# A decoder block's gated recurrence: TensorE's order in the heads written out, VectorE's share in pieces, keys by a backward scan

## The chip, the cores and the metric

The kernel runs on one core of a Trainium2 chip, whose engines (TensorE, VectorE, ScalarE, GpSimd and SyncE) each work through an instruction stream of their own in order and wait for each other by semaphores. The metric is the device time of one execution in microseconds; the time of a kernel is the median of several executions.

## The reference

One decoder block for a sequence of 1024 tokens, 1024 channels wide, all in float32:

```python
proj = x @ w_in          # -> q, f, i, o_gate, pool_v, gate_a, gate_b
qf = silu(q) * 128 ** -0.5
f  = lb + (1 - lb) * sigmoid(f_pre);  k = 1 - f
# per head, 8 heads of 128: S_t = diag(f_t) S_{t-1} + k_t v_t^T ;  o_t = S_t^T q_t
o = hgrn2_chunked(qf, k, i, log f)
a = (rms_norm(o) * hgrn_norm_g * sigmoid(o_gate)) @ w_a
b = per_group_linear(causal_mean_w(pool_v) - pool_v) * pool_scale     # windows 2, 4, 8, 16
x = layer_norm(alpha * x + (sigmoid(gate_a) * a + sigmoid(gate_b) * b) @ w_out)
x = layer_norm(alpha * x + relu(x @ w_up) ** 2 @ w_down)
```

The recurrence is a scan over tokens, but inside a chunk it can be written with matrix products of queries, keys and values, each scaled by products of the decays `f` from the chunk's start to the token or from the token to the chunk's end.

## The kernel before

Every large product is made of three TensorE products of rounded parts (a high and a low part of each operand: high x high, high x low, low x high), and 2x2 block products are made of seven block products in place of eight. `pair` describes such a set of seven: two weight blocks of 128 columns against the two halves (512 tokens each) of the input. Each of its steps makes a weight operand (`w_part`: ScalarE rounds it to the high part, line 118, VectorE subtracts for the low part, line 119) and then issues 12 matmuls of 128x512 (`prod`, lines 201 to 204) into one PSUM bank. Sums between banks are taken by `copied` and `added` (lines 271 and 275). The weight operands sit in a ring of ten tiles, `w`. `run` issues the steps of a pair one after the other.

The heads stage runs after the value columns of the first projection. Its pairs are `head_inputs(h)` (q and f of head h), `output_gates(h)` (gates of two heads), `gates(j)` (the two merge gates) and `pooled(g)` (pooled input of group g, with its running means on VectorE). Between them stands `hgrn(h, u, ...)`, the recurrence of head h, half u (512 tokens, four chunks of 128, sub-blocks of 16):

- VectorE scans `f` forward within each sub-block for the running decay `fd` (line 811), takes its reciprocal (line 817), and makes from them the scaled queries and keys; ScalarE copies parts of them; GpSimd makes the small tables of decays (`T`, `p32`, `p64`, `dec`, `eq`, `ek`).
- TensorE transposes the keys to the chunk's end (line 870), forms the chunk states (line 875), the scores (lines 887 and 898) and the outputs (lines 915 and 918). VectorE chains the states (line 883) and copies the scores under a mask into `att` (line 905).
- ScalarE makes the norm (lines 923, 924 and 928, with a reciprocal on VectorE at line 925); TensorE transposes the result back (line 931), VectorE multiplies it by the gate in tile `og` (line 932), and SP's queue writes it to DRAM as `o` (line 933).

Tiles come from rings with a fixed number of buffers, named in `RINGS`; a new tile waits until the last use of the oldest one in its ring is over. All loads and stores of this stage are issued by SyncE (SP) in its own order. `o_sums(kp)` loads four finished halves of `o`, makes four sums and stores them.

After the last head come `pool_products(g)`, for g = 0 to 3: for each half it loads two pooled blocks (into rings `og` and `v`), splits them, and multiplies them with the group's pool weights (24 matmuls of 128x512 a group, lines 105 to 107). `gates(5)` to `gates(7)` are traced among them. Then the merge begins (products with `w_a`, then `w_out`, the layer norms and the MLP), which the change leaves alone.

What sets the order: the kernel is traced in program order, and a scheduler orders the instructions of each engine by the time that its own model foresees, with priorities where the kernel gives them. So before the change the recurrence's small matmuls fall between the matmuls of the pairs wherever the scheduler puts them.

Of the kernel before, what the change touches and what calls it, by code (L numbers as in the profile page):

```python
# [9 lines left out]
F32 = mybir.dt.float32  # L10
# [6 lines left out]
P = 128  # L17
# [12 lines left out]
PRIO_LAST = 3000  # L30
# [13 lines left out]
def tile_hybrid_block(  # L44
# [311 lines left out]

    def run(*pairs, made=(), behind=()):


        for i, steps in enumerate(zip(*pairs)):  # L360
            made_now = list(made[i]) if made else []
            if made_now:
                made_now.pop(0)()
            with tc.issue_after(made_last[behind[i]]) if behind and behind[i] else nullcontext():
                ws = [{operand: operand() for operand in operands} for operands, _ in steps]
            for n in range(len(ws[0])):
                if made_now:
                    made_now.pop(0)()
                for w, (_, products) in zip(ws, steps):
                    operand, product = products[n]  # L370
                    product(w[operand])

# [245 lines left out]
    with tc.tile_pool(name="tmp", bufs=1, side="right", reuse_waits="tile") as tmp:  # L618
# [3 lines left out]
        att = [hgp.tile([P, CH, P], F32, name=f"att{i}") for i in range(1)]  # L622
        for t in att:
            G.memset(t, 0.0)
# [6 lines left out]
        RINGS = dict(q=3, f=3, og=2, v=2, tA=2, tC=2, st=2)  # L631
# [11 lines left out]
        def head_inputs(h, behind=()):  # L643
            fs, qs = [None, None], [None, None]
# [23 lines left out]
            return fs, qs  # L668
# [39 lines left out]
        def pool_products(g):  # L708
# [6 lines left out]
            raw = raw_tile().rearrange("p k n c -> p (k n c)")[:, : 2 * 2 * P].rearrange("p (k c) -> p k c", c=2 * P)  # L715
# [90 lines left out]
        def hgrn(h, u, ft, q, v, og, state):  # L806

            fd = tt("tA")
            for i in range(2):
                w = slice(i * QUARTER, (i + 1) * QUARTER)  # L810
                V.tensor_tensor_scan(fd[:, w], starts.rearrange("p b s -> p (b s)"), ft[:, w], 1.0, ALU.max, ALU.mult)
            k = ft
            A.activation(k, ft, AF.Identity, bias=cmask[:, P - 1 : P], scale=-1.0)
            r = tt("tC")
            for i in range(CH):
                w = slice(i * P, (i + 1) * P)
                V.reciprocal(r[:, w], fd[:, w])  # L817
            T = small("T", [P, NB])
            G.tensor_copy(T, blk(fd)[:, :, SUB - 1])
            T2 = T.rearrange("p (b e) -> p b e", e=2)  # L820
            p32 = small("p32", [P, CH, 4])
            p32f = p32.rearrange("p c b -> p (c b)")
            G.tensor_mul(p32f, T2[:, :, 0], T2[:, :, 1])
            p64 = small("p64", [P, CH, 2])
            p32p = p32f.rearrange("p (b e) -> p b e", e=2)
            G.tensor_mul(p64.rearrange("p c e -> p (c e)"), p32p[:, :, 0], p32p[:, :, 1])
            dec = small("dec", [P, CH])
            G.tensor_mul(dec, p64[:, :, 0], p64[:, :, 1])
            eq = small("eq", [P, CH, 4])
            G.memset(eq[:, :, 0:1], 1.0)  # L830
            G.tensor_copy(eq[:, :, 1], p32[:, :, 0])
            G.tensor_copy(eq[:, :, 2], p64[:, :, 0])
            G.tensor_mul(eq[:, :, 3], p64[:, :, 0], p32[:, :, 2])
            ek = small("ek", [P, CH, 4])
            G.memset(ek[:, :, 3:4], 1.0)
            G.tensor_copy(ek[:, :, 2], p32[:, :, 3])
            G.tensor_copy(ek[:, :, 1], p64[:, :, 1])
            G.tensor_mul(ek[:, :, 0], p64[:, :, 1], p32[:, :, 1])


            V.tensor_mul(q, q, fd)
            kc = tt("tD")
            V.tensor_mul(kc, k, r)
            kr = tt("tE")
            V.tensor_mul(blk(kr), blk(kc), bc(T, [P, NB, SUB]))
            A.copy(pairs_of(kc)[:, :, 0], pairs_of(kr)[:, :, 0])
            qc = tt("tF")
            A.copy(pairs_of(qc)[:, :, 1], pairs_of(q)[:, :, 1])
            V.tensor_mul(
                pairs_of(qc)[:, :, 0], pairs_of(q)[:, :, 0],  # L850
                bc(pairs_of(r)[:, :, 0, SUB - 1], [P, NB // 2, SUB]),
            )
            V.tensor_mul(pairs_of(q)[:, :, 1], pairs_of(q)[:, :, 1], bc(T2[:, :, 0], [P, NB // 2, SUB]))
            V.tensor_mul(pairs_of(kr)[:, :, 0], pairs_of(kr)[:, :, 0], bc(T2[:, :, 1], [P, NB // 2, SUB]))
            q64 = hgp.tile([P, CH, 2, 32], F32, tag="q64", name=nm("q64"))
            k64 = hgp.tile([P, CH, 2, 32], F32, tag="k64", name=nm("k64"))
            A.copy(q64[:, :, 0], half64(q, 1)[:, :, 0])
            V.tensor_mul(q64[:, :, 1], half64(q, 1)[:, :, 1], bc(p32[:, :, 2], [P, CH, 32]))
            A.copy(k64[:, :, 1], half64(kr, 0)[:, :, 1])
            V.tensor_mul(k64[:, :, 0], half64(kr, 0)[:, :, 0], bc(p32[:, :, 1], [P, CH, 32]))  # L860
            qi = tt("tA")
            b32 = lambda t: t.rearrange("p (b s) -> p b s", s=32)
            V.tensor_mul(b32(qi), b32(q), bc(eq.rearrange("p c b -> p (c b)"), [P, 16, 32]))
            ke = tt("tC")
            V.tensor_mul(b32(ke), b32(kr), bc(ek.rearrange("p c b -> p (c b)"), [P, 16, 32]))


            pt = ps_tile("tr", 2)
            for c in range(CH - u):
                PE.transpose(pt[:, c * P : (c + 1) * P], ke[:, c * P : (c + 1) * P], ident)  # L870
            ket = tt("tH")
            A.copy(ket[:, : (CH - u) * P], pt[:, : (CH - u) * P])
            ds = ps_tile("hg", 2)
            for c in range(CH - u):
                PE.matmul(ds[:, c * P : (c + 1) * P], ket[:, c * P : (c + 1) * P], v[:, c], start=True, stop=True)
            st = tt("st")
            for c in range(CH - u):
                o = st[:, c * P : (c + 1) * P]
                if state is None and c == 0:
                    V.tensor_copy(o, ds[:, 0:P])  # L880
                else:
                    prev = state[:, 3 * P :] if c == 0 else st[:, (c - 1) * P : c * P]
                    V.scalar_tensor_tensor(o, prev, dec[:, c : c + 1], ds[:, c * P : (c + 1) * P], ALU.mult, ALU.add)


            def score(part, lo, keys, queries):
                PE.matmul(sc[part : part + 32, lo : lo + queries.shape[-1]], keys, queries, start=True, stop=True)

            for c in range(CH):
                for b in range(4):  # L890
                    lo = c * P + b * 32
                    score(b * 32, lo, kc[:, lo : lo + 32], qc[:, lo : lo + 32])
            for c in range(CH):
                for b in (0, 2):
                    lo = c * P + b * 32
                    score(b * 32, lo + 32, kr[:, lo : lo + 32], q[:, lo + 32 : lo + 64])
            for c in range(CH):
                PE.matmul(
                    sc[0:64, c * P + 64 : (c + 1) * P],
                    k64[:, c].rearrange("p a b -> p (a b)"),  # L900
                    q64[:, c].rearrange("p a b -> p (a b)"),
                    start=True, stop=True,
                )
            at = att[(2 * h + u) % 1]
            V.copy_predicated(
                at, cmask.bitcast(U32).unsqueeze(1).to_broadcast([P, CH, P]),
                sc.rearrange("p (c t) -> p c t", t=P),
            )


            o = ps_tile("hg", 2)
            for c in range(CH):
                w = slice(c * P, (c + 1) * P)
                first = state is None and c == 0
                PE.matmul(o[:, w], at[:, c], v[:, c], start=True, stop=first)
                if not first:
                    prev = state[:, 3 * P :] if c == 0 else st[:, (c - 1) * P : c * P]
                    PE.matmul(o[:, w], qi[:, w], prev, start=False, stop=True)
            ss = small("ss", [P, CH])
            on = tt("tH")  # L920
            for c in range(CH):
                w = slice(c * P, (c + 1) * P)
                A.activation(on[:, w], o[:, w], AF.Square, accum_out=ss[:, c : c + 1])
            A.activation(ss, ss, AF.Sqrt, bias=eps_rms, scale=1.0 / P)
            V.reciprocal(ss, ss)
            for c in range(CH):
# [20 lines left out]
        for h in range(HEADS):  # L947
            fs, qs = nxt
            state = None
            for u in range(2):  # L950
# [6 lines left out]
                if h + 1 < HEADS and u:  # L957
                    nxt = head_inputs(h + 1)
                    if h % 2:
                        output_gates(h + 1)  # L960
# [441 lines left out]
```

## Time and profile before

| | |
|---|---|
| median of 3 runs | 1462.83 us (1462.3 to 1464.97) |
| profiled execution | 1460.19 us |
| its span, first to last instruction | 1458.5 us |
| mean granted TensorE clock | 0.996 |
| heads stage, about | 118 to 600 us |

The profile is of one execution. Line numbers in it are those of the kernel before. "PE" is TensorE, "DVE" VectorE, "ACT" ScalarE, "POOL" GpSimd and "SP" SyncE; `out<-in` names the tiles that an instruction writes and reads; the number before a comma in a group's row is its busy time in us, the one behind it the mean duration in ns.

### The profile page before, as it was taken

The numbers are of one execution on the slowest core, as the hardware profiler recorded it, in microseconds if no ns is written. First come the engines' busy times: TensorE is split into PE (matmuls) and PEld (weight loads), VectorE is DVE, ScalarE is ACT, GpSimd is POOL, SyncE is SP. The second block draws the span as 40 slices with busy tenths as digits, with TensorE's granted clock in tenths as the row PEclk, the third lists the DMA queues.
The fourth block names the chain that finished last, engine by engine and source line by source line (L and its number), as shares of the span: only waits on it lengthen the run. The fifth ranks groups of instructions, "written<-read, shape, count | busy, mean of one in ns | idle before, by whom it ended". The sixth has DMA issues, their size and how long they took to land.

```text
span 1458.5 us, 20662 instructions
## 1 busy us (share of the span) xinstructions
PE 1436.4 (98%) x7377; PEld 1187.9 (81%) x7377; DVE 1141.6 (78%) x1838; ACT 758.3 (52%) x1383; POOL 58.6 (4%) x244
## 2 busy tenths in 40 slices
PE   8999999999999998999999999999999999999997
PEld 7888888888888886788888878888888888888886
DVE  5967989899898885768985597666666787777977
ACT  5445565666656655556542376555555443333535
POOL 0001001001000010000002100000000100000000
PEclk9999999999999999999999999999999999999999
DMA  7232233323234447897672225444474874445322
GB/s 253 70 126 87 85 98 101 109 75 114 90 99 138 152 132 249 301 299 241 223 247 99 73 94 195 159 146 144 152 261 149 275 260 150 153 141 163 130 73 116
DMA packets 160615, 226.82 MB, mean 156 GB/s; under 512 B 11232, under 2 KB 84480, under 8 KB 160512
## 3 DMA queue, kind: packets, MB, share of 16 engines
q1 hardware_dynamic: 158576, 218.93, 44.7%
q0 software_dynamic: 1152, 4.19, 0.8%
q10 hardware_dynamic: 784, 2.38, 0.5%
q8 instruction: 58, 0.95, 0.3%
q14 instruction: 45, 0.37, 0.1%
HBM read 154.16 MB, written 71.30 MB: 155 GB/s over the span
## 4 chain that ended last, share of the span: by engine, by line
PE 94%; DVE 3%; DMA 1%; ACT 1%; issue 0%; SPq 0%; DVEq 0%
PE ps_pj L201 16%; PE ps_pj L203 16%; PE ps_pj L204 16%; PE ps_pj L1283 4%; PE ps_pj L1285 4%; PE ps_pj L1284 4%; PE ps_pj L106 3%; PE ps_pj L107 3%; PE ps_pj L105 2%; PE ps_tr L1285 1%; PE ps_tr L1283 1%; PE ps_tr L1284 1%; PE ps_sc L201 1%; PE ps_sc L203 1%; PE ps_sc L204 1%; PE ps_hg L203 1%
## 5 line engine op out<-in xcount | busy, mean ns | idle before, releaser
L201 PE MATMUL ps_pj<-act,w 128*128 128x512 f32 x1068 | 421.6, 395 | 0.4 <-ACT act L123 0.2
L203 PE MATMUL ps_pj<-act,w 128*128 128x512 f32 x1068 | 415.1, 390 | 0.5 <-DVE act L124 0.5
L204 PE MATMUL ps_pj<-act,w 128*128 128x512 f32 x1068 | 414.1, 390 | 0.0
L201 PEld LDWEIGHTS ps_pj<-act,w 128*128 128x128 f32 x1068 | 200.6, 188 | 42.8 <-ACT act L123 0.6
L204 PEld LDWEIGHTS ps_pj<-act,w 128*128 128x128 f32 x1068 | 200.5, 188 | 42.3
L203 PEld LDWEIGHTS ps_pj<-act,w 128*128 128x128 f32 x1068 | 200.6, 188 | 40.6 <-DVE act L124 0.9
L118 ACT CAST w<-t 128x512 fp32r<-128x512 f32 x170 | 104.7, 620 | 105.0 <-PE ps_pj L203 53.8
L118 ACT CAST w<-raw 128x512 fp32r<-128x512 f32 x143 | 88.2, 620 | 117.3 <-PE ps_pj L203 62.5
L119 DVE TENSOR_TENSOR w<-raw,w 128x512 fp32r<-128x512 f32 x143 | 99.8, 702 | 55.2 <-ACT w L118 53.9
L119 DVE TENSOR_TENSOR w<-t,w 128x512 fp32r<-128x512 f32 x170 | 115.9, 685 | 29.6 <-ACT w L118 29.4
L1245 ACT CAST act<-act 128x1024 fp32r<-128x1024 f32 x66 | 66.9, 1050 | 107.9 <-issue 35.0
L1246 DVE TENSOR_TENSOR act<-act,act 128x1024 fp32r<-128x1024 f32 x66 | 79.3, 1220 | 18.5 <-ACT act L1245 15.8
L1285 PE MATMUL ps_pj<-act,act 128*128 128x512 f32 x240 | 92.9, 389 | 0.0
L1284 PE MATMUL ps_pj<-act,act 128*128 128x512 f32 x240 | 92.9, 389 | 0.0
L1283 PE MATMUL ps_pj<-act,act 128*128 128x512 f32 x240 | 92.4, 389 | 0.0
L275 DVE TENSOR_TENSOR c<-c,ps_pj 128x512 f32<-128x512 f32 x95 | 64.5, 681 | 18.0 <-PE ps_pj L204 13.4
L271 ACT COPY c<-ps_pj 128x512 f32<-128x512 f32 x96 | 55.2, 582 | 12.8 <-PE ps_pj L204 12.8
L817 DVE RECIPROCAL tC<-tA 128x128 f32<-128x128 f32 x64 | 54.1, 904 | 0.0
L1284 PEld LDWEIGHTS ps_pj<-act,act 128*128 128x128 f32 x240 | 45.1, 188 | 9.4
L1285 PEld LDWEIGHTS ps_pj<-act,act 128*128 128x128 f32 x240 | 45.1, 188 | 9.4
L1283 PEld LDWEIGHTS ps_pj<-act,act 128*128 128x128 f32 x240 | 45.1, 188 | 9.3
L241 DVE TENSOR_TENSOR t<-raw,raw 128x512 f32<-128x512 f32 x43 | 29.6, 689 | 21.9 <-DMA raw<-in_w_in_dram 19.7
(415 smaller groups left out, 2719.8 us busy)
## 6 DMA issues: line engine op xcount, KB each, us to landing
h<-c SPq DMA_DIRECT2D x106, 256.0 KB, 2.1
act<-h SPq DMA_DIRECT2D x78, 256.0 KB, 2.9
raw<-in_w_in_dram SPq DMA_DIRECT2D x64, 256.0 KB, 3.4
draw<-in_w_down_dram SPq DMA_DIRECT2D x16, 1024.0 KB, 7.8
raw<-in_w_up_dram SPq DMA_DIRECT2D x30, 512.0 KB, 4.2
raw<-in_w_in_dram SPq DMA_DIRECT2D x18, 512.0 KB, 4.0
hf<-h SPq DMA_DIRECT2D x34, 256.0 KB, 2.9
c<-o SPq DMA_DIRECT2D x24, 256.0 KB, 3.4
```

Of the source, the lines that this page charges most:

```text
L118: A.copy(hi, src)
L119: V.tensor_sub(lo, src, f(hi))
L201: PE.matmul(ps, wh[:, k], th, start=first and k == 0, stop=False, skip_group_check=True)
L203: PE.matmul(ps, wh[:, k], tl, start=False, stop=False, skip_group_check=True)
L204: PE.matmul(ps, wl[:, k], th, start=False, stop=k == CH - 1, skip_group_check=True)
L271: A.copy(t, ps)
L275: V.tensor_add(t, t, ps)
L1245: A.copy(hi, src)
L1246: V.tensor_sub(lo, src, f(hi))
L1283: PE.matmul(ps, hh[:, w], wh, start=fresh and n == 0, stop=False, skip_group_check=True)
L1284: PE.matmul(ps, hh[:, w], wl, start=False, stop=False, skip_group_check=True)
L1285: PE.matmul(ps, hl[:, w], wh, start=False, stop=n == M - 1, skip_group_check=True)
```

## The change

1. **Recurrence in parts.** `hgrn` becomes a class `Half` with methods: `prepare` (VectorE's, ScalarE's and GpSimd's share, a generator in six pieces), `turn_keys`, `scores`, `far_queries`, `states`, `load`, `outputs`, `turn_outputs`. A generator `recurrence` steps through all 16 halves. For half n TensorE's work stands in two groups: first the outputs of half n-1 with the key transposes and scores of half n, then four turns later the output transposes of n-1 with the states of n.
2. **TensorE's order.** After `head_inputs(0)` the rest of the stage is traced under a manual schedule for TensorE: its instructions keep the order in which they are traced. `run` advances the recurrence by one turn after each product of a pair; a half takes 8.5 turns on the mean. `ORDER` lists the pairs. After `ORDER` and the last turns come `pool_products(0)`, `gates(6)`, `pool_products` 1 to 3 and `gates(7)`.
3. **Keys by a backward scan.** The decay from each token to its sub-block's end, `to_end`, is scanned from `f` with negative steps; the keys are `k * to_end`. The four reciprocals of 128 columns and two products of 512 columns go; a reciprocal of the 32 sub-block ends and a product of 256 columns come.
4. **Rings.** `f` 3 to 4, `og` 2 to 1, `tC` 2 to 1, `tH` 1 to 2; the pool weights are loaded to a `tA` tile, not to a `raw` tile.
5. The raised priority of the last half goes.

```diff
-PRIO_LAST = 3000
+PER_HALF = 8.5
+TURN_BACK = 4
+TURNS_AHEAD = 3
+ORDER = (
+    ("inputs", 1), ("pooled", 0), ("inputs", 2), ("gates", 0), ("output_gates", 2), ("inputs", 3), ("pooled", 1),
+    ("inputs", 4), ("output_gates", 4), ("gates", 1), ("inputs", 5), ("pooled", 2), ("inputs", 6), ("output_gates", 6),
+    ("gates", 2), ("inputs", 7), ("pooled", 3), ("gates", 3), ("gates", 4), ("gates", 5),
+)
...
                     product(w[operand])
+                    next(turning[0], None)
...
-        RINGS = dict(q=3, f=3, og=2, v=2, tA=2, tC=2, st=2)
+        RINGS = dict(q=3, f=4, og=1, v=2, tA=2, tH=2, st=2)
...
-            raw = raw_tile().rearrange("p k n c -> p (k n c)")[:, : 2 * 2 * P].rearrange("p (k c) -> p k c", c=2 * P)
+            raw = tt("tA").rearrange("p (k c) -> p k c", c=2 * P)
...
-            r = tt("tC")
-            for i in range(CH):
-                w = slice(i * P, (i + 1) * P)
-                V.reciprocal(r[:, w], fd[:, w])
...
-            V.tensor_mul(kc, k, r)
-            kr = tt("tE")
-            V.tensor_mul(blk(kr), blk(kc), bc(T, [P, NB, SUB]))
...
+                V.tensor_tensor_scan(
+                    to_end[:, HALF - 2 : QUARTER - 1 : -1], ft[:, HALF - 1 : QUARTER : -1], first_of[:, 1:],
+                    1.0, ALU.mult, ALU.max,
+                )
+                V.tensor_tensor_scan(
+                    to_end[:, QUARTER - 1 :: -1], ft[:, QUARTER : 0 : -1], first_of, 0.0, ALU.mult, ALU.max,
+                )
...
+                V.reciprocal(rT, blk(fd)[:, :, SUB - 1])
...
+                V.tensor_mul(kr, k, to_end)
...
+                V.tensor_mul(pairs_of(kc)[:, :, 1], pairs_of(kr)[:, :, 1], bc(rT2[:, :, 1], [P, NB // 2, SUB]))
...
+            for n in range(2 * HEADS + 1):
+                if old:
+                    old.outputs()
+                if now:
+                    now.turn_keys()
+                    now.scores()
+                yield
+                if now:
+                    now.far_queries()
+                nxt = half(n + 1, now) if now else None
+                pieces = nxt.prepare() if nxt else iter(())
+                at += PER_HALF
+                for turn in range(1, round(at) - round(at - PER_HALF)):
+                    if turn == TURN_BACK:
+                        if old:
+                            old.turn_outputs()
+                        if now:
+                            now.states()
+                        if nxt:
+                            nxt.load()
+                        if old and old.u and old.h >= CH:
+                            last = old.h == HEADS - 1
+                            tags = iter(("tD", "tE", "tF", "tC"))
+                            o_sums(old.h - CH, (lambda: tt(next(tags))) if last else c_tile)
+                    else:
+                        next(pieces, None)
+                    yield
+                for _ in pieces:
+                    pass
+                now, old = nxt, now
...
+        with tc.manual_schedule(engines={mybir.EngineType.PE}):
+            turns = turning[0] = recurrence()
+            output_gates(0)
+            for what, j in ORDER:
+                if what == "inputs":
+                    head_inputs(j)
                 else:
+                    dict(gates=gates, pooled=pooled, output_gates=output_gates)[what](j)
+            for _ in turns:
+                pass
+            for what, j in (
+                ("pool_products", 0), ("gates", 6), ("pool_products", 1), ("pool_products", 2), ("pool_products", 3), ("gates", 7),
+            ):
+                dict(gates=gates, pool_products=pool_products)[what](j)
```

More of the change, by code (lines that the diff above doesn't have):

```diff
@@ L355, in pair @@
         )
+    turning = [iter(())]
     def run(*pairs, made=(), behind=()):
@@ L621, in tile_hybrid_block @@
         G.memset(starts[:, :, 0:1], 1.0)
-        att = [hgp.tile([P, CH, P], F32, name=f"att{i}") for i in range(1)]
-        for t in att:
-            G.memset(t, 0.0)
+        att = hgp.tile([P, CH, P], F32, name="att")
+        G.memset(att, 0.0)
         hg_tags.remove("sc")
@@ L804, in bc @@
             return a.unsqueeze(len(a.shape)).to_broadcast(shape)
[L806 to L813, printed above, removed]
-            r = tt("tC")
-            for i in range(CH):
-                w = slice(i * P, (i + 1) * P)
[L817 to L843, printed above, removed]
-            kr = tt("tE")
[L845 to L880, printed above, removed]
-                else:
[L882 to L926, printed above, removed]
-                w = slice(c * P, (c + 1) * P)
-                A.activation(on[:, w], o[:, w], AF.Copy, scale=ss[:, c : c + 1])
-            pt = ps_tile("tr", 2)
-            for c in range(CH):
-                PE.transpose(pt[:, c * P : (c + 1) * P], on[:, c * P : (c + 1) * P], ident)
-            V.scalar_tensor_tensor(og, pt, g_col[:, h : h + 1], og, ALU.mult, ALU.mult)
-            nc.sync.dma_start(out=od[h][u], in_=og)
-            return st
@@ L946, in tile_hybrid_block, with chunk @@
[L946 to L962 removed]
+        def chunk(c):
+            return slice(c * P, (c + 1) * P)
```

167 lines of the change are left out of this document (147 added, 20 removed).

## The prediction

> **What bounds the kernel now.** I read the page's head first, then the chain that ended last, then busy time by stretches.
>
> ```profile
> span 1458.5 us, 20662 instructions
> PE 1436.4 (98%) x7377; PEld 1187.9 (81%) x7377; DVE 1141.6 (78%) x1838; ACT 758.3 (52%) x1383; POOL 58.6 (4%) x244
> PE 94%; DVE 3%; DMA 1%; ACT 1%; issue 0%; SPq 0%; DVEq 0%
> ```
>
> TensorE (PE) is the bound: 98% busy and 94% of the chain. Something that only lightens another engine gains nothing by itself. The change touches the heads stage, so I asked for busy time in that stage (columns: stretch, its length, then busy us and count for PE, PEld, DVE, ACT, POOL, then granted clock, DMA share, GB/s).
>
> ```profile
> 160.00:560.00 400.00, 400.00 (x2643) 332.48 (x2642) 360.11 (x705) 242.96 (x548) 29.14 (x170) 1.00 0.36 115
> 570.00:580.00 10.00, 6.98 (x44) 5.75 (x42) 5.09 (x9) 5.68 (x17) 0.00 (x0) 1.00 0.57 182
> 580.00:590.00 10.00, 7.11 (x20) 4.82 (x20) 4.10 (x7) 6.54 (x13) 0.00 (x0) 0.66 0.66 222
> 600.00:610.00 10.00, 10.00 (x45) 8.03 (x44) 4.94 (x8) 6.85 (x11) 0.00 (x0) 1.00 1.03 336
> ```
>
> From 160 to 560 us TensorE has no idle time. VectorE has 40 us of it, so it isn't the bound, though it is close. The one hole is at the end of the heads, between 570 and 590 us. TensorE's waits name it (who waited for whom: us, times, longest):
>
> ```profile
> PE ps_pj L105 <- ACT w L118: 4.7, 1, 4.7
> PE ps_hg L915 <- DVE st L883: 1.2, 1, 1.2
> PE ps_pj L106 <- DVE w L119: 0.8, 1, 0.8
> ```
>
> and the chain of waits shows what stands behind the 4.7 us (start, us, what):
>
> ```profile
> 573.53 2.31 DMA o<-og
> 577.18 4.97 DMA og<-po
> 582.18 0.62 ACT w L118
> ...
> 586.19 0.43 PE ps_pj L107
> ...
> 591.47 0.23 PE ps_pj L107
> ```
>
> A finished half of the recurrence is written out of an `og` buffer (`o<-og`); only then can that buffer take the first pooled block of `pool_products(0)` (`og<-po`), which ScalarE rounds before TensorE may start. After the wait the clock is at 0.66, and matmuls of 512 columns come every 0.43 us in place of 0.23: some 14 of them until 589 us, 14 x 0.20 = 2.8 us. So the hole costs 1.2 + 4.7 + 0.8 + 2.8 = 9.5 us. That is all idle time the change can touch.
>
> **The change part by part.**
>
> *The recurrence as one stream.* The same matmuls stand in another order. In the program before, those of the 16 halves stand in 67 separate groups among the 128x512 products, in the changed one in 34. What a group costs beyond its own matmuls (start, duration, line):
>
> ```profile
> 362.65 0.39 PE L204 MATMUL ps_pj<-act,w 128*128 128x512 f32 x1
> 362.97 0.68 PE L898 MATMUL sc<-q,k 128*64 128x64 f32 x8
> 363.58 0.50 PE L201 MATMUL ps_pj<-act,w 128*128 128x512 f32 x1
> 363.91 0.39 PE L203 MATMUL ps_pj<-act,w 128*128 128x512 f32 x1
> ...
> 372.54 0.40 PE L204 MATMUL ps_pj<-act,w 128*128 128x512 f32 x1
> 372.77 1.06 PE L875 MATMUL ps_hg<-v,tH 128*128 128x128 f32 x8
> 373.58 0.47 PE L201 MATMUL ps_pj<-act,w 128*128 128x512 f32 x1
> 373.90 0.39 PE L203 MATMUL ps_pj<-act,w 128*128 128x512 f32 x1
> ```
>
> Starts of 128x512 products lie 0.227 us apart in a row. From the product before the group to the second one behind it are 1.26 us; less two steps (0.45) and the 0.61 us from the group's first start to the next product, that leaves 0.20 us. The second group leaves 1.36 - 0.45 - 0.81 = 0.10. Merging saves this where two groups share a border, and nothing where each kind of matmul brings its own gap. 33 groups fewer at 0 to 0.20 us: 0 to 6.6 us, and I take the row with 0.10, 3.3 us.
>
> *Keys by a backward scan.* (Columns: busy us, mean ns.)
>
> ```profile
> L817 DVE RECIPROCAL tC<-tA 128x128 f32<-128x128 f32 x64 | 54.1, 904 | 0.0
> L811 DVE TENSOR_TENSOR_SCAN tA<-starts,f 128x256 f32<-128x256 f32 x32 | 20.3, 672 | 1.1 <-PE ps_hg L918 1.1
> L843 DVE TENSOR_TENSOR tD<-f,tC 128x512 f32<-128x512 f32 x16 | 10.9, 683 | 0.0
> L845 DVE TENSOR_TENSOR tE<-tD,T 128x512 f32<-128x512 f32 x16 | 10.9, 683 | 0.0
> L849 DVE TENSOR_TENSOR tF<-q,tC 128x256 f32<-128x256 f32 x16 | 6.7, 417 | 0.0
> ```
>
> Out, for each half: four reciprocals, 54.1/16 = 3.4 us, and both products of 0.68: 4.75 us. In: two backward scans, one product of 0.68, one of 256 columns at 0.42, and a reciprocal of 32 columns. A scan that runs backward is in no row: at least the 0.42 of any operation of 256 columns, at most the 1.8 of a reciprocal of as many; I take the forward scan's 0.67. The small reciprocal: 32/128 of 0.90, 0.23. In: 2.67 us. VectorE loses about 2.1 us a half, 33 us in all; by the ends of the scan's bounds from 3 us more to 42 less. TensorE waits for VectorE nowhere in this stage, so this is worth nothing to the time, and it is cover: if the pieces were to bind, these 33 us come off first.
>
> *VectorE's pieces against a fixed order.* TensorE can no longer take what is ready. I added up VectorE's own work in the changed order between one copy of the scores and the next, by the durations in the rows, against TensorE's products in between. A half gives TensorE 26 to 29 us; VectorE has 20 to 37, the most where `pooled(2)` and `pooled(3)` fall. The operands that VectorE prepares are due at least 5.7 us after its own work for them is done. What can eat that lead is the load of the next weights:
>
> ```profile
> DVE t L241 <- DMA raw<-in_w_in_dram: 19.7, 12, 3.5
> ```
>
> at most 3.5 us each. 2.2 us are left, so I cost this at nothing. If the lead is gone, each of the four `pooled` stretches shows it on TensorE.
>
> *One `og` buffer in place of two, and the order of the tail.* Here I expect the time to go. In the changed order the last half's outputs stand ahead of two products, then come its transposes, then at once `pool_products(0)`, which must start with a block in `og`. `gates(6)` stands behind that on TensorE and can't be pulled ahead. Rows for the chain:
>
> ```profile
> L932 DVE SCALAR_TENSOR_TENSOR og<-ps_tr,prm,og 128x512 f32<-128x512 f32 x16 | 11.9, 745 | 0.2 <-PE ps_tr L931 0.2
> o<-og SPq DMA_DIRECT2D x16, 256.0 KB, 2.1
> og<-po SPq DMA_DIRECT2D x8, 256.0 KB, 3.9
> L118 ACT CAST w<-og 128x512 fp32r<-128x512 f32 x8 | 5.0, 620 | 4.9 <-DMA og<-po 3.2 <-issue 1.0 <-PE ps_pj L203 0.5
> DMA to landing us min/median/max: 2.7/3.9/7.9
> ```
>
> (The last is the view of tile `og` from 556 to 660 us: issue to landing.) The norm's work on ScalarE lies under the two products. From the transposes on nothing covers: VectorE 0.75, the store 2.3 as in the chain, the `o_sums` load that stands ahead on SP's queue 0.35 (it waits for that store, and SP with it), the load 3.9, the cast 0.62, hand-overs 0.5: 8.4 us idle, by the landing's ends 7.2 to 12.4. Then the half clock, 2.8 us as before. The second half's block can be loaded only when the first is split, so some 0.8 us more. First stop: 12.0 us.
>
> Next, `pool_products` 1, 2 and 3 stand in a row, 24 matmuls each, 5.45 us, two `og` blocks each. With one buffer a block takes a full round: landing 3.9, cast 0.62, subtraction 0.69, queue 0.3 = 5.5 us, against 2.7 us of matmuls. The ring of ten `w` tiles lets the first block's cast begin three products, 8.2 us, before TensorE reaches group 1; it is done at -7.6, and a round each later the second at -2.1, the third (group 2) at 3.4, the fourth at 8.9. ScalarE's order puts the rounding of group 2's weights behind that fourth cast and one more: 8.9 + 1.2 = 10.1, where TensorE is free at 5.45. Second stop: 4.7 us, half clock again, 2.8; and 0.7 at the next group, whose weights wait for the buffer of the last: 8.2, with 0.7 for SP's entries in between 8.9 us. By the landing's ends this stop is 1.8 to 20 us; DMA runs at a share of 1.03 there.
>
> *The sum.* The profiled execution took 1460.2 us, 1.7 over its span. 1460.2 - 9.5 (the old hole) - 3.3 (groups) + 12.0 + 8.9 = 1468.3. The median of the three runs is 2.6 above this execution: 1470.9.
>
> On the clock the Trainium skill has a rule of its own, in "TensorE: Matmul & The Clock Gate", Part 1: the gate closes to half after an idle window of about 3.4 us and opens after about as long a busy one. The trace agrees on the closing: 4.7 us of waiting closed it, 1.2 us left it at 1.00. By the page a restart would cost an estimated 1.7 us at least in place of 2.8, and the two of them 2.2 us less. The page speaks against this change, as it trades one such wait for two.
>
> **The rivals.**
>
> *The blocks land fast.* At 2.7 us for each landing the first stop is 7.2 + 2.8, the second 1.1 us, too short for the clock, and 0.7: 11.8. 1460.2 - 9.5 - 3.3 + 11.8 + 2.6 = 1461.8, not slower; with groups at 0.20 us 1458.5. It decides at a round of 4.3 us. For it: 2.7 is in the row, and TensorE's stop leaves DMA less to share. Against: the median, and the share of 1.03.
>
> *VectorE becomes the bound at the pooled heads.* If its lead of 2.2 us is gone, TensorE waits 2 to 4 us at each of four stretches: 8 to 16 on top, about 1483. For it: 37 us against 28.7 at the worst half. Against: no such wait before, with 33 us more to do.
>
> *The order does not do what it says.* TensorE had no idle time in the heads; if merged groups keep each kind's gap, nothing comes back and the tail stands: 1474.2.
>
> **How the numbers follow.** The forecast, 1471, has 0.52 (its own range 1465 to 1479); fast blocks 0.28; VectorE 0.12; no gain from the order 0.08. What a measurement can tell from no change is 0.2%, 2.9 us: faster is below 1459.9, slower above 1465.8. Of the fast blocks 0.19 lie below and 0.09 within; of the forecast 0.03 within; all else is above. Faster 0.19, same 0.12, slower 0.69. The range reaches to the fast case with the better groups and to the VectorE case: 1458 to 1483.
>
> **What would show it.** Right: no idle time on TensorE in the heads; a wait of 7 us or more at the first product of `pool_products(0)`, released by ScalarE's cast of `og`, with the store and the load in the chain before it and a clock well under 1 behind it; a second wait of some 5 us between groups 1 and 2. VectorE's busy time down by about 33 us. Wrong: the first wait under 5 us or none at group 2 (then 1461 or less), waits for VectorE's splits in the heads, or another stage changed in length.

## The result, and the profile after

The changed kernel takes 1476.9 us (median of four, 1475.4 to 1478.5), the kernel before 1462.6 us in the runs beside it: ratio 1.0098, 95% interval 1.0085 to 1.0110. That is 14.3 us slower, where 8.1 were forecast. The profiled execution of the changed kernel took 1478.5 us; its span is 18.0 us longer than that of before, 3.7 us more than the medians differ: the profiled execution is the slowest of the four after, and of before the profile is of a fast one.

The head of the page after:

```profile
span 1476.5 us, 20702 instructions
PE 1439.8 (98%) x7377; PEld 1191.5 (81%) x7377; DVE 1113.2 (75%) x1822; ACT 759.3 (51%) x1383; POOL 82.3 (6%) x260
PE 86%; DVE 6%; DMA 5%; ACT 2%; issue 1%; SPq 0%; DVEq 0%; ACTq 0%
```

VectorE is 28.4 us less busy (1141.6 before), and yet it and DMA have grown from 4% to 11% of the chain that ended last. TensorE is busy 3.4 us more and idle 36.7 us in place of 22.1. An engine's share of the span, 98% as before, doesn't show this; the list of TensorE's waits does (who waited for whom: us, times, longest; in the changed kernel lines 112 to 114 are the pool's matmuls, 208 to 211 those of `prod`, 125 and 126 the split of a weight, 278 `copied`, 282 `added`):

```profile
PE ps_pj L112 <- ACT w L125: 7.6, 1, 7.6
PE ps_pj L208 <- ACT c L278: 6.0, 2, 5.6
PE ps_pj L112 <- ACT q L125: 3.4, 2, 3.0
PE ps_pj L208 <- DVE c L282: 1.9, 1, 1.9
...
PE ps_pj L114 <- DVE f L126: 1.0, 2, 0.8
```

Four stops, then. Busy time by stretches says where, and what the clock did behind each (columns as in the prediction):

```profile
118.00:140.00 22.00, 20.06 (x81) 16.10 (x81) 16.15 (x31) 10.29 (x19) 6.92 (x16) 0.92 0.34 109
160.00:540.00 380.00, 378.24 (x2557) 317.13 (x2556) 313.53 (x643) 232.49 (x526) 50.59 (x178) 1.00 0.35 112
540.00:560.00 20.00, 17.99 (x86) 14.63 (x84) 18.48 (x45) 10.37 (x21) 1.24 (x7) 1.00 0.54 172
560.00:570.00 10.00, 6.36 (x16) 4.99 (x17) 6.09 (x10) 2.32 (x4) 0.00 (x0) 0.66 0.63 212
570.00:600.00 30.00, 30.00 (x204) 25.48 (x203) 12.75 (x22) 14.71 (x32) 0.00 (x0) 1.00 0.54 175
600.00:620.00 20.00, 12.41 (x49) 9.28 (x48) 7.91 (x14) 9.91 (x24) 0.00 (x0) 0.83 0.58 188
...
640.00:660.00 20.00, 15.52 (x58) 11.43 (x57) 10.70 (x17) 6.15 (x11) 0.00 (x0) 0.91 0.93 318
```

The old hole between 570 and 590 us is gone (30.00 of 30). The two stops of the tail are there, after 600 and after 640 us. Two more were not forecast: one near 130 us and one near 560 us. Behind each of the four the granted clock is under 1 for a while.

**The tail**, from the chain of waits (start, us, what):

```profile
607.34 2.47 DMA o<-og
...
610.19 2.89 DMA og<-po
613.11 0.63 ACT w L125
...
613.78 0.80 PE ps_pj L112
...
643.02 4.63 DMA og<-po
...
649.10 4.69 DMA og<-po
...
655.23 3.35 DMA og<-po
```

Store, load into the same buffer, cast, first product: the first stop link by link as forecast, 7.6 us idle. Its matmuls then come 0.43 us apart until 617.5 us, which costs 2.2 us against steps of 0.23. Between 640 and 660 us the loads into the one buffer follow each other a round of some 6 us apart (643.02, 649.10, 655.23); there TensorE is idle 4.5 us in four waits (15.52 busy of 20), and loses 1.7 us to the clock.

**At 130 us.** VectorE's own timeline, and TensorE's first matmul behind the stop:

```profile
125.20 0.69 DVE L248 TENSOR_TENSOR t<-raw,raw 128x512 f32<-128x512 f32 x1 [2.66 <-DMA raw<-in_w_in_dram]
125.81 0.68 DVE L248 TENSOR_TENSOR t<-raw 128x512 f32<-128x512 f32 x1
126.41 1.26 DVE L833 TENSOR_TENSOR_SCAN tA<-starts,f 128x256 f32<-128x256 f32 x2
...
129.34 0.34 DVE L847 RECIPROCAL rT<-tA 128x32 f32<-128x32 f32 x1
...
130.75 0.68 DVE L282 TENSOR_TENSOR c<-c,ps_pj 128x512 f32<-128x512 f32 x1
...
131.48 0.50 PE L208 MATMUL ps_pj<-act,w 128*128 128x512 f32 x1 [1.94 <-DVE c L282]
```

A block of weights lands late; VectorE stands at it, and behind it come the scans and products of the first half of the recurrence, and only then the addition (line 282) that gives TensorE its PSUM bank back. 1.94 us of waiting, and 1.7 us at the lower clock.

**At 560 us.** VectorE, ScalarE and TensorE around the stop (lines 617 to 620 are the four sums of `o_sums`):

```profile
560.01 0.69 DVE L617 TENSOR_TENSOR c<-c,c 128x512 f32<-128x512 f32 x1 [1.24 <-DMA c<-o]
...
563.00 0.59 ACT L278 COPY c<-ps_pj 128x512 f32<-128x512 f32 x1 [4.58 <-DVE c L619]
...
563.64 0.79 PE L208 MATMUL ps_pj<-act,w 128*128 128x512 f32 x1 [5.65 <-ACT c L278]
```

TensorE waits for a PSUM bank, ScalarE's copy out of that bank waits for a tile `c`, and that tile is held by `o_sums(2)`, which VectorE had only begun at 560.01, when its last load landed: four of the six `c` buffers are in its hands. SP issued its four loads at 540.4 (two), 551.5 and 557.1 us, so the first buffers stood taken for some 20 us before a sum began, and VectorE itself stood idle 1.24 us for the last. `recurrence` now puts `o_sums(2)` at a fixed turn of the half in which `pooled(3)` runs, and VectorE has 18.48 us of 20 to do there. 5.65 us idle, 2.9 at the lower clock.

### The profile page after: what moved, and what is told of

It is laid out like the page before. It is cut to its first block, busy times and chain, and to the rows that moved or that the text cites. A ratio compares the mean times of both kernels' runs of the same rounds, so it can differ in the third digit from the quotient of the medians.

```text
span 1476.5 us, 20702 instructions
## 1 busy us (share of the span) xinstructions
PE 1439.8 (98%) x7377; PEld 1191.5 (81%) x7377; DVE 1113.2 (75%) x1822; ACT 759.3 (51%) x1383; POOL 82.3 (6%) x260
## 4 chain that ended last, share of the span: by engine, by line
PE 86%; DVE 6%; DMA 5%; ACT 2%; issue 1%; SPq 0%; DVEq 0%; ACTq 0%
PE ps_pj L208 14%; PE ps_pj L210 14%; PE ps_pj L211 14%; PE ps_pj L1360 4%; PE ps_pj L1361 4%; PE ps_pj L1359 4%; PE ps_pj L113 2%; PE ps_pj L112 2%; PE ps_pj L114 2%; PE ps_tr L1360 1%; PE ps_tr L1361 1%; PE ps_tr L1359 1%; PE ps_sc L208 1%; DMA og<-po 1%; PE ps_sc L211 1%; PE ps_sc L210 1%
## 5 line engine op out<-in xcount | busy, mean ns | idle before, releaser
L1225 ACT ACTIVATE c<-c 128x512 f32<-128x512 f32 x61 | 38.6, 633 | 1.7
```

## The experiments

Each ratio is against the kernel before (median 1462.6 to 1463.4 us in the sets of runs), with its 95% interval. To compare two variants I take the difference of their ratios times 1463 us; the changed kernel stands at 1.0098. Such a difference carries the intervals of both ratios and is uncertain by 2 to 4 us.

### The buffer of the pooled blocks

```diff
-            tags = iter(("q", "f", "og", "v") * 3)
+            tags = iter(("q", "f", "tH", "v") * 3)
```

> The changed kernel with the pooled blocks of pool_products in the ring tH (two buffers, the oldest of them free before the last half's store) in place of the single og buffer; all else stays. Theory (one buffer): both stops at the end of the heads come from it, 7.6 + 2.8 + 0.6 us at the first and about 4.5 + 1.7 at the second; both go, and the time falls by 14 to 17 us, to 1460 to 1463. Rival (the transfers themselves are the limit, at a share of the DMA engines near 1, whatever buffer they go to): the first stop goes, the second stays or grows, and the time falls by 6 to 11 us, to 1466 to 1471. Rival (the wait moves to the next thing that the store held up, such as the o_sums load): under 5 us.

Measured: 1472.4 us, 1.0057 (1.0036 to 1.0077), 6.0 us less than the changed kernel (2.5 to 9.5). Busy time of the tail, and two links of its chain:

```profile
600.00:620.00 20.00, 19.39 (x87) 15.26 (x87) 12.62 (x21) 12.46 (x29) 0.00 (x0) 1.00 0.76 251
620.00:640.00 20.00, 18.62 (x81) 14.76 (x80) 13.88 (x23) 9.56 (x17) 0.00 (x0) 1.00 0.93 308
640.00:660.00 20.00, 17.91 (x69) 14.03 (x70) 13.11 (x22) 10.55 (x19) 0.00 (x0) 0.91 1.00 333
660.00:680.00 20.00, 17.41 (x77) 14.08 (x77) 13.44 (x21) 9.25 (x17) 0.00 (x0) 1.00 0.69 241
```

```profile
643.07 4.55 DMA pb<-f
...
655.17 7.20 DMA pb<-q
```

The first stop is gone (19.39 of 20, clock 1.00): it was the single `og` buffer. The second is not shorter: from 620 to 680 us TensorE is idle 6.1 us, where it was 4.5, and other transfers now end last there: stores of results, 4.6 and 7.2 us, that free the `f` and `q` buffers, with the DMA engines at a share of 1.00. So the rival holds: the first stop goes, the second stays or grows, and its lower figure, 6 us, is what was measured. Whether the transfers as such or their order on SP's queue set the second stop, this run can't tell. The stop near 560 us was 6.5 us long in this run, a little longer than before.

### Where the sums stand

All three early `o_sums` one half later:

```diff
-                        if old and old.u and old.h >= CH:
+                        if old and old.h >= CH:
...
+                            if not old.u and old.h > CH:
+                                o_sums(old.h - 1 - CH)
```

> The changed kernel with o_sums for heads 4, 5 and 6 one half later, so that none falls into the stretch of pooled(3); the last one stays. Theory (the stop of 5.65 us at 558 us comes from VectorE standing at the load of o_sums while ScalarE and then TensorE wait for the buffer behind it): it goes with its half clock, and the time falls by 7 to 9 us, to 1468 to 1470. Rival (VectorE is simply full with the means of pooled(3), which my prediction named as a rival): TensorE still waits there, 4 us or more with the half clock, and the time changes by under 3 us.

Measured: 1491.3 us, 1.0188 (1.0168 to 1.0207): 13 us slower than the changed kernel, which neither the theory nor the rival had. TensorE's timeline:

```profile
550.69 0.79 PE L208 MATMUL ps_pj<-act,w 128*128 128x512 f32 x1 [11.16 <-ACT c L278]
```

The move took the sums of head 6 out of the stretch of `pooled(3)` and put those of head 5 into it. The same wait, for the same kind of buffer, is now twice as long. The next run moves one only:

```diff
-                        if old and old.u and old.h >= CH:
+                        if old and (old.h, old.u) in ((4, 1), (5, 1), (7, 0), (7, 1)):
```

> The changed kernel with one thing moved: o_sums of head 6 stands one half later, so that its four c buffers are not taken while VectorE works on pooled(3); those of heads 4, 5 and 7 stay. Theory (the stop at 558 us is ScalarE's copy for gates(3) waiting for a c buffer that o_sums holds, while VectorE gets to the sums only between the means of pooled(3)): the stop of 5.65 us and its 2.8 us of half clock go, and the time falls by 7 to 9 us from 1476.9, to 1468 to 1470. Rival (VectorE full with the means is enough by itself): the stop shrinks by VectorE's 2.8 us for the sums at most, under 4 us. Rival (the sums only collide elsewhere, as when all three were moved): no gain or a loss.

Measured: 1474.6 us, 1.0073 (1.0056 to 1.0091), 3.7 us less than the changed kernel; the profiled execution, the shortest of four, is 7.8 us shorter in span. Busy time there:

```profile
540.00:560.00 20.00, 20.00 (x96) 16.68 (x95) 18.25 (x43) 10.59 (x20) 0.00 (x0) 1.00 0.44 138
560.00:570.00 10.00, 10.00 (x104) 8.54 (x103) 5.67 (x10) 8.04 (x21) 0.00 (x0) 1.00 0.76 254
```

No idle time and no lower clock, with VectorE as busy as before (18.25 of 20). So the stop came from `o_sums` holding the buffers, and VectorE's load alone doesn't make it. But the gain isn't kept whole: the first stop of the tail is 8.8 us long in this profile, not 7.6, and the other three executions took 3.9 to 5.0 us more than the profiled one, for which no trace shows the place. In the profiled one the stop near 130 us happened to be 1.0 us long, with the clock at 1.00 behind it, 2.6 us less than in the changed kernel's profile, though the edit doesn't touch it; so of its 7.8 us some 5 belong to the edit.

Both edits together:

> The changed kernel with only two of the three edits: the ring tH for the blocks, and o_sums of head 6 one half later. Alone the ring was worth 5 us and the sums 4. Theory (each of them alone hands part of its gain to the next stop, together they don't): 1463 to 1465, that is 2.4 us above c2_all for the start at 131 us. Rival (plain sum of the single effects): 1476.9 - 5.2 - 3.6 = 1468.

Measured: 1462.6 us, 1.0002 (0.9993 to 1.0011), just below the theory's 1463 to 1465. The two edits bring 14.0 us, the whole loss, where alone they bring 6.0 and 3.7. The 4.3 us by which both exceed the sum are no larger than their interval (4.5 us either way); what the profiles show of it is that the other stop grew when one was taken away, from 5.65 to 6.5 us and from 7.6 to 8.8. Nor is the end of the heads free of stops now: TensorE waits 0.9 us for the last half's transposes and 2.1 us at the first pooled product, and the clock is at 0.83 from 590 to 610 us. The chain of waits leads there from the sums of head 6 in their new place, over a copy and the norm of the last half; no run tests this.

### The start

```diff
-            for _ in now.prepare():
+            for _ in range(4):
                 yield
-            for _ in range(TURNS_AHEAD):
-                yield
+            with tc.issue_after(adds[-1]): [_ for _ in now.prepare()]
+            for _ in range(4): yield
```

(`adds` collects the additions of line 282.)

> The changed kernel with the preparation of the first half of head 0 put behind the first addition of output_gates(0) on VectorE; the first keys are turned at the same place of TensorE's order as before. Theory (the stop of 1.9 us at 129 to 131 us comes from that addition standing behind about 4 us of the first half's pieces, after a block of weights that landed late): it goes with the half clock behind it, the time falls by 3.5 to 5 us, to 1472 to 1473.5. Rival (the late block of weights alone delays TensorE): the stop stays at its place with 1 us or more, under 1 us of change. Miss on the other side: the pieces are now late for the first scores and the stop only moves.

Measured: 1477.6 us, 1.0097 (1.0080 to 1.0113), no change. Busy time at the start and at 540 us:

```profile
118.00:140.00 22.00, 20.69 (x144) 16.89 (x142) 17.14 (x33) 12.12 (x24) 7.22 (x18) 1.00 0.33 99
540.00:560.00 20.00, 15.49 (x75) 12.59 (x73) 17.14 (x41) 8.28 (x16) 0.00 (x0) 0.94 0.46 148
```

The wait for the addition is gone and the clock stays at 1.00, but the pieces, pushed back, are late for the first transposes by 1.3 us, and the stop near 560 us is 7.1 us long in place of 5.65. With the other two edits:

> The changed kernel with three edits together: pool_products' blocks in the ring tH, o_sums of head 6 one half later, the first half's preparation behind the first addition of output_gates(0). By the sum of single effects: 1476.9 less 4.5 (ring, measured), 8.4 (sums, expected), 2.4 (start: what the stretch from 120 to 140 us showed, lost again at 558 us in that run) = 1461.6, the same as before the change. Rival (stops move on to the next collision): above 1467. What would be left against before, if the theory holds, is the second stop of the tail, some 8 us in stores of the products that free their buffers late.

Measured: 1461.7 us, 0.9993 (0.9982 to 1.0005). That is the sum in the expectation to 0.1 us, but its terms were not right one by one: with two edits alone the time is already at 1.0002, and the third is worth 1.3 us, within what the intervals leave open. So the agreement of the sum is luck. The stop at the end of the heads is here too, 3.25 us idle:

```profile
580.00:600.00 20.00, 16.75 (x79) 13.00 (x78) 7.00 (x13) 9.22 (x23) 0.00 (x0) 1.00 0.59 197
```

One turn more before the first transposes:

```diff
-PER_HALF = 8.5
+PER_HALF = 8.4375
...
-            for _ in range(4): yield
+            for _ in range(5): yield
```

> The three edits of c2_all, the first keys turned one product later, the pace a shade faster (8.4375 products a half in place of 8.5) so that the recurrence ends at the same product. Theory (the stop of 1.3 us at the first transposes, before 139 us, is VectorE a little late with the last piece of the first half): it goes, 1 to 1.5 us less than c2_all. Rival (the faster pace brings a half with 9 products down to 8 at a pooled head, and a stop there takes the gain): no change or more.

Measured: 1461.9 us, 0.9995 (0.9986 to 1.0004). The wait of 1.3 us is gone from the profile; the time is the same within some 2 us, so the 1 to 1.5 us expected can be neither seen nor excluded.

### The backward scan

Keys by reciprocals again, in the changed kernel, then the same with the three edits:

```diff
-                to_end = tt("tC")
+                r = tt("tC")
...
+                for i in range(CH):
+                    V.reciprocal(r[:, chunk(i)], fd[:, chunk(i)])
...
-                V.tensor_mul(kr, k, to_end)
+                V.tensor_mul(kc, k, r)
+                V.tensor_mul(blk(kr), blk(kc), bc(T, [P, NB, SUB]))
```

> The changed kernel with the keys by reciprocals again (the scan to the end of the block undone), all else as changed. By my prediction the backward scan takes about 2 us a half from VectorE and is worth nothing to the time by itself. Theory (cover only, TensorE waits for other things): VectorE is busy 28 to 33 us more, and the time stays within 3 us, 1474 to 1480. Rival (in the fixed order VectorE is close to binding and the scan holds it open): TensorE waits for VectorE at the pooled heads and at the start, 2 us or more each, and the time rises by 8 to 20 us, to 1485 to 1497.

Measured: 1494.0 us, 1.0217 (1.0193 to 1.0242), 17.4 us slower than the changed kernel; VectorE is busy 31.4 us more. TensorE's waits:

```profile
PE ps_pj L208 <- ACT c L278: 17.5, 3, 11.9
PE ps_pj L112 <- ACT w L125: 7.7, 1, 7.7
```

The waits for a `c` buffer, 6.0 us in the changed kernel, are 17.5: 11.9 us at `o_sums(2)`, 5.4 at `o_sums(0)`, which had none (there the buffer that came free at last was one of a pooled mean, by its store). So the rival's time holds, and these 11.5 us more, two thirds of the loss, sit where sums and means meet: at two of the four pooled heads.

> The three edits together, with the keys by reciprocals again. Theory (the reciprocals' 30 us of VectorE hurt only where sums and means already meet, at 445 and 560 us): the loss against the same kernel with the scan is half of the 17 us measured without the edits, 5 to 9 us, and it sits at 445 us. Rival (in the written order VectorE binds all along with the reciprocals): 15 us or more, spread over the stretches. Rival (the scan is worth nothing once the sums are out of the way, as my prediction had it): under 2 us.

Measured: 1474.9 us, 1.0077 (1.0060 to 1.0093), 12.3 us slower than with the scan, more than the theory's 5 to 9 and less than the rival's 15. Two stretches of this kernel, both of which are 20.00 of 20 at a clock of 1.00 with the scan:

```profile
140.00:160.00 20.00, 17.57 (x125) 14.68 (x126) 19.15 (x36) 9.61 (x19) 5.47 (x14) 0.84 0.19 54
440.00:460.00 20.00, 14.58 (x59) 11.69 (x58) 16.37 (x37) 6.14 (x12) 0.10 (x1) 0.83 0.55 184
```

The stop after 445 us is the one expected (5.4 us idle in one wait for a `c` buffer, and the clock at 0.83). The other is new: with the longer preparation behind the first addition, the first transposes came 4.65 us late. In the written order the scan's 30 us are needed in a few places, not all along.

The scan alone, in `hgrn` of the kernel before:

```diff
-            r = tt("tC")
-            for i in range(CH):
-                w = slice(i * P, (i + 1) * P)
-                V.reciprocal(r[:, w], fd[:, w])
+            to_end = tt("tC")
...
-            V.tensor_mul(blk(kr), blk(kc), bc(T, [P, NB, SUB]))
+            V.tensor_mul(kr, k, to_end)
```

> The kernel before with the backward scan alone: VectorE 30 us less busy, TensorE's order left to the scheduler. My prediction costs this at nothing: within 1.5 us of before. Rival (VectorE's ends decide the hole of the tail, or the order that the scheduler picks): 3 us or more, either way.

Measured: 1464.0 us, 1.0014 (1.0004 to 1.0024): 2.0 us slower, with 29.4 us less of VectorE. Its waits:

```profile
PE sc L907 <- DVE k L869: 2.9, 2, 1.7
...
PE ps_pj L105 <- ACT c L696: 1.9, 1, 1.9
PE ps_pj L201 <- ACT w L118: 1.6, 1, 1.6
PE ps_hg L924 <- DVE st L892: 1.4, 1, 1.4
```

```profile
580.00:600.00 20.00, 15.42 (x66) 11.98 (x67) 11.38 (x21) 10.81 (x25) 0.00 (x0) 0.91 0.62 208
```

That is between the theory's 1.5 us and the rival's 3. The wait of 4.7 us before the pooled products is no longer there, but shorter ones stand in its place (4.6 us idle from 580 to 600, with the clock at 0.91), and small waits have come earlier that the kernel before didn't have, two of them for the keys. TensorE's order in the two traces is not the same: removing work from an engine that TensorE hardly waits for changed the order that the scheduler chose, and the new one is no better.

### What is left in the tail

```diff
-                ("pool_products", 0), ("gates", 6), ("pool_products", 1), ("pool_products", 2), ("pool_products", 3), ("gates", 7),
+                ("pool_products", 0), ("pool_products", 1), ("gates", 6), ("pool_products", 2), ("pool_products", 3), ("gates", 7),
```

> The three edits of c2_all, and gates(6) moved from ahead of pool_products 1 to between 1 and 2, so that no three groups stand in a row. Theory (what is left in the tail, 3.4 us between 630 and 660 us, is transfers that two buffers can't bring in time while three groups run in a row, at a share of the DMA engines near 1; the 32.7 us of gates(6) in their midst let them catch up): the stop there is under 1 us and the time falls by 2 to 3 us from 1461.7, below before the change. Rival (the blocks of the second group are now wanted at once behind the first, and the stop moves ahead of it, with a half clock): the same or slower by up to 4 us.

Measured: 1461.5 us, 0.9994 (0.9985 to 1.0004), the same as with the three edits alone (0.9993). Busy time with the moved pair:

```profile
600.00:620.00 20.00, 17.91 (x64) 13.10 (x63) 15.57 (x25) 7.16 (x13) 0.00 (x0) 0.88 0.95 333
620.00:640.00 20.00, 20.00 (x90) 16.56 (x89) 12.94 (x21) 9.67 (x18) 0.00 (x0) 1.00 0.91 305
640.00:660.00 20.00, 18.93 (x82) 15.05 (x81) 16.31 (x27) 13.48 (x25) 0.00 (x0) 1.00 1.01 352
```

The 2.3 us of idle time between 620 and 640 us are gone, and 2.1 us have come between 600 and 620 (0.5 without the move): the rival's outcome. (`gates(6)` takes 19 us of TensorE, 621.5 to 640.9 us in the changed kernel, not the 32.7 of the expectation.)

The last run takes the wait of the old hole by itself, in the kernel before:

```diff
-            tags = iter(("q", "f", "og", "v") * 3)
+            tags = iter(("q", "f", "og" if g else "tA", "v") + ("q", "f", "og", "v") * 2)
```

> The kernel before, with its scheduler's order, and one buffer changed: the first pooled block of pool_products(0) goes to the ring tA in place of og. Theory (the old hole of 9.5 us is one block waiting for a buffer that the store of half 14 holds, the same kind of wait as the changed kernel's first stop): the 4.7 us, the 2.8 us of half clock and some of the 2.0 us around them go, and the time falls by 6 to 9 us from 1462.8, to 1454 to 1457, below both kernels. Rival (the last half, which these products covered badly, now stands bare behind them): the hole only moves, under 3 us of gain. Rival (the tail's transfers start earlier and collide at a share near 1): a stop between 600 and 660 us takes half of it.

Measured: 1464.8 us, 1.0013 (1.0004 to 1.0022), 1.9 us slower. The chain and TensorE's timeline:

```profile
576.52 2.22 DMA o<-og
...
580.12 5.62 DMA og<-po
```

```profile
586.43 1.22 PE L105 MATMUL ps_pj<-w,q 128*128 128x512 f32 x2 [8.10 <-ACT w L118]
```

The first block comes early now. The next block, of the second half, takes the `og` buffer that the first one had waited for, and waits for the same store. The wait is 8.1 us in place of 4.7: the store begins 3.0 us later than before (576.52 for 573.53) and the load takes 5.6 us for 5.0, while TensorE's order puts two of the waiting products ahead of the last half's outputs. Why the store begins later is not shown. So the old hole was a wait for that store, but one block's buffer only hands it on: the first rival's outcome, the hole moves. No version run here is measurably faster than the kernel before.

## Why the prediction was right and wrong

Point by point, with the profiled executions' numbers:

- **TensorE as the bound, and the old hole.** Right: the hole is gone, 9.5 us.
- **Merged groups, 3.3 us.** What the points below add (14.0 in the heads, 9.8 and 6.2 in the tail) and a wait of 0.7 us behind it, less the old hole, sum to 21.2 us; the span grew by 18.0, which leaves 3.2 for the groups and what else TensorE gained. A count over TensorE's timelines agrees: where each kernel does the scores of 14 halves (160 to 560 us before, 160 to 540 after), the time beside waits and steps of 0.227 us for the 128x512 matmuls is 70.8 us before and 67.4 after. So the rival by which nothing comes back doesn't hold. No run has the merged groups alone.
- **The backward scan.** Its price was right (0.67 us for a backward scan), VectorE's gain a little too high: 28.4 us, not 33; the reciprocal of 32 columns, 0.34 us where I had 0.23, explains some 2 of the 5 us, and the rest is open. "Worth nothing to the time" was wrong in the changed kernel: there it is worth 17 us, because the pieces do bind, and it was right as cover, as the same sentence says. ("TensorE waits for VectorE nowhere in this stage" overlooks the 1.2 and 0.8 us in its own list, at the stage's end; from 160 to 560 us there are none.) In the kernel before it costs 2 us.
- **VectorE's pieces against a fixed order, costed at nothing.** This is the step that failed: of the signs of being right, "no idle time on TensorE in the heads" didn't come, with 8.6 us at 560 us, 3.6 us at 130 us, and 1.8 us of small waits from 160 to 540 us, 14 us together. I compared VectorE's work between two copies of the scores with TensorE's products. That count holds: with the sums of head 6 moved, the fullest stretch runs without idle time. What it left out is what else stands in VectorE's queue and holds buffers: `o_sums`, which I put into the tail alone, on SP's queue, though the diff places three of them in the heads at fixed turns (before, they ran at 488, 541 and 578 us, and TensorE waited for no `c` buffer there); and the start, where the lead has not yet been built up. I asked when operands are ready, and not when buffers come free. The rival "VectorE becomes the bound at the pooled heads" had the place right, but one stretch instead of four, and another mechanism.
- **The first stop of the tail.** Every link was right: 7.6 us idle for 8.4 forecast. The half clock cost 2.2 us, not 2.8, and the 0.8 us for the second half's block didn't come: 9.8 us for 12.0. The run with the blocks in another ring shows the cause.
- **The second stop.** There, and shorter: 4.5 us idle and 1.7 of clock, 6.2 for 8.9, though its loads took 4.6 and 4.7 us where I used 3.9. The loads into the single buffer end its waits, as forecast, but my cause is not shown: with two buffers alone TensorE is idle no less from 620 to 680 us (6.1 us for 4.5), and stores that free `q` and `f` end the waits.
- **The sum.** The tail was 5 us too dear (11.4 forecast with the old hole taken off, 6.5 measured) and the heads 14 us too cheap. The direction came out because the tail by itself, with the groups taken off, would have made the kernel some 3 us slower; that the time is no further from the forecast is luck, as the two errors have opposite signs.

The clock rule that I cited, "TensorE: Matmul & The Clock Gate", Part 1, of the Trainium skill, speaks of an idle window of about 3.4 us. Here 1.94 us was enough, so the trace differs from the page; a stop of that length has to be costed with its clock. The 1.7 us at least that I worked out from the page for a restart fit the four stops, which lost 1.7, 2.9, 2.2 and 1.7 us.

## What to carry to other kernels

When an order is written by hand, cost every instruction that the new place puts in front of a buffer's release, not only those that make operands: list for each ring who holds it at the fullest moment and which queue the holder stands in. When several stops follow one another, expect a fix of one to give part of its gain to the next, and try the fixes together before judging any (6.0 and 3.7 us alone, 14.0 together, though the 4.3 us between them are no larger than their interval). Work on an engine that is 75% busy and releases the bound engine's buffers can cost time of its own: here 30 us of VectorE's work less were worth 17 us in one order, 12 in the same order mended, and nothing in another.

## What the hardware showed that I had not expected

TensorE's granted clock fell to half after waits much shorter than the 4.7 us in the profile before. Waits on TensorE, without those in the first 10 us of the program, and whether the matmuls of 512 columns behind them came 0.43 us apart (or, where other matmuls stood there, the granted clock fell), over all profiles here:

| wait, us | half clock behind it |
|---|---|
| up to 1.69, standing alone | never |
| 1.79 (one case) | no |
| 1.86 (one case) | yes |
| 1.94 and 1.95 (three cases) | yes, each time |
| 2.07 to 2.32 (eight cases) | yes, each time |
| 2.33 and 2.59 (one case each) | no |
| 2.95 and more | yes, each time |

Between 1.8 and 2.6 us it goes both ways, and nothing here shows what decides. The single wait isn't all that counts: five of the eight cases from 2.07 to 2.32 us stand a few us behind a wait of 0.6 to 0.9 us, and a wait of 1.02 us that stood 1.8 us behind one of 0.48 was followed by the half clock too. The lower pace doesn't always start with the first matmul either: after the wait that ended at 131.48 us the next matmuls came 0.23 to 0.37 us apart, and the slow ones ran from 133.1 to 136.1 us. A stop of 1.94 us so cost 1.7 us more.

A scan with negative steps costs the same as a forward one:

```profile
L833 DVE TENSOR_TENSOR_SCAN tA<-starts,f 128x256 f32<-128x256 f32 x32 | 20.3, 675 | 2.1 <-PE ps_hg L963 2.1
...
L841 DVE TENSOR_TENSOR_SCAN tC<-f,starts 128x256 f32<-128x256 f32 x16 | 10.6, 664 | 0.0
```
